# Layer 0's FFN in seven block products: where its weight sums are formed, and where layer 1's

## The chip, the cores and the metric

One core of one Trainium2 chip runs the whole program. The time is device microseconds of that core. The kernel before took 1684.92 us, the median of three runs (1684.33 to 1690.12). A core has TensorE (PE in the profile), VectorE (DVE), ScalarE (ACT), GpSimd (POOL) and SyncE (SP), which issues the DMA transfers here.

## The reference

Two layers. Each has a token mixer of four parallel head groups (spatial gating, a bidirectional recurrence, windowed attention, pooling) between an input and an output projection, and then a SwiGLU FFN. X is 512 tokens of 1024 channels, the context C 256 tokens; layer 1 no longer updates C. All is fp32. What matters here is the FFN, with a hidden width of 2816, and the modulation, which gives shift, scale and gate of each layer from one vector:

```python
FFN_HIDDEN = -(-(8 * D_MODEL) // (3 * 256)) * 256     # 2816

def modulate(h, shift, scale):
    return h * (1 + scale) + shift
...
def swiglu(h, w_in_, w_out_):
    gate, up = jnp.split(h @ w_in_, 2, axis=-1)
    return (jax.nn.silu(gate) * up) @ w_out_
...
    x = x + g_f * rms_norm(swiglu(modulate(rms_norm(x, norm_g[2]), sh_f, sc_f), w_ffn_in, w_ffn_out), norm_g[3])
```

## The kernel before

**Matmuls.** Weights and activations are split into a high and a low part, and one fp32 product is three matmuls (`mac3`: high by high, high by low, low by high). A hidden tile of 128 of the 2816 channels needs two weight units of 1024 x 128, one for gate and one for up; the kernel calls it a pair, and there are 22, numbered from 0. In dense form a pair is 2 x 8 x 3 = 48 matmuls of 512 columns.

**Seven block products.** In layer 1 (`'strassen': (1,)`), pairs 4 to 21 take another form: the gate and up weights are seen as a matrix of 2 x 2 blocks, the tokens as 2 x 2 blocks of half the channels and half the tokens (`Quarters`), and seven block products replace eight. A product is 4 x 3 matmuls of 256 columns, so a pair is 84 of these. The right sides of the products are formed once (`strassen_rhs`, L1513). The left sides need four sums of weight blocks per pair, each 128 x 512. They don't depend on activations, so the kernel forms all 18 pairs' sums early, in layer 0's FFN (`weight_sums`, L1541), and stores them in DRAM (`ws`): per pair four loads of 256 KB into buffers `sa_m`, four adds at L1556 (`'sad': 'PPVV'`, two on POOL and two on DVE) and four stores of 256 KB at L1565. `strassen_pair` (L1574) then loads them like weights.

**Weights.** All streamed weights go through a ring of seven buffers `wr` (128 x 1024, 512 KB), loaded from SP's queue, then ACT writes the high part `wh` (L408) and DVE or POOL the low part `wl` (L409). Prefetched units that are held go into `wt_m`.

**Background work.** `weights` and `strassen_pair` call `tick` (L455) for each unit, which adds `bg_rate` to a counter and runs a queued task for each whole 1. In layer 0's FFN the queue holds 32 tasks of layer 1's modulation (`mods_sums`; each one `wmod` load of 512 KB and two DVE accumulations `macc_m`, L675 and L677) with the sums' tasks strewn among them, at `bg_rate` 1.4 (`rate2`). What is left is run by `flush`, which `then` in `layer_end` calls ahead of layer 1's first norm, since that norm needs the modulation.

**Order.** A scheduler with a timeline of its own places the instructions of each engine, within the priorities that the program sets; each engine then runs its own list in order. SP's list holds every load and store, so a store that waits for an add holds up the loads behind it.

**Stages by the profile's time:** to about 100 us the start; 100 to 570 layer 0's X projection and mixers, with the context's FFN woven in; 570 to 690 the output projection and norm; 690 to 1049 layer 0's FFN; 1049 to 1062 the norm into layer 1; to 1300 layer 1's projection and mixers, among them the recurrence, whose head norm takes `bym` from POOL (L504); 1313 to 1672 layer 1's FFN. In the norm, `rmsv` (L561) and `rmsy` (L504) are the root mean squares, `rs_t` (L595) the gated branch, `sq_t` and `sq_m` (L529) the squares that are added up, `y` (L1456) the FFN's output tiles; "halves" are tiles of 256 of the 512 tokens.

The two lines that set the rate and the mix of tasks, in `mix` of `run`:

```python
            for i, f in enumerate(b):
                self.bg += a[i * len(a) // len(b):(i + 1) * len(a) // len(b)] + [f]
            self.bg_rate = T["rate2"]
```

Of the kernel before, what the change touches and what calls it, by code (L numbers as in the profile page):

```python
# [66 lines left out]
 'rate2': 1.4,  # L67
# [41 lines left out]
 'strassen': (1,),  # L109
 'fcs': ((0, 4), (4, 7), (7, 11), (11, 16), (16, 22)),  # L110
 'fco': 4,
 'fcp': (5, 1, 3),
 'wq': 2,
 'sad': 'PPVV',
 'slo': 'PVVPPVP',
# [147 lines left out]
class Build:  # L263
    def __init__(self, tc, es, I, out, dbg=None):
# [22 lines left out]
        self.sums = {}  # L287
        self.pre = deque()
# [1252 lines left out]
    def weight_sums(self, l, j0, j1):  # L1541

        nc = self.nc

        def load(j, box):
            for u in range(2):
                for v in range(2):
                    s = self.main.get("sa")
                    nc.sync.dma_start(out=s.t[:, 0:512].rearrange("p (a b) -> p a b", b=P), in_=self.I["wfi"][l, j, u][:, v * 4:v * 4 + 4])
                    box.append(s)  # L1550

        def form(j, box):
            a11, a12, a21, a22 = (s.t[:, 0:512] for s in box)
            box += [self.main.get("sb") for _ in range(2)]
            s1, s2 = (s.t[:, 0:512] for s in box[4:])
            tt = lambda c, o, a, b, op=ALU.subtract: self.e(c).tensor_tensor(out=o, in0=a, in1=b, op=op)  # L1556
            e = T["sad"]
            tt(e[0], s1, a21, a22, ALU.add)
            tt(e[1], a21, a11, a21)
            tt(e[2], s2, s1, a11)  # L1560
            tt(e[3], a12, a12, s2)
            d = self.dr.tile([P, 2, KT, P], F32, tag=f"ws{l}{j}", name=f"ws{l}{j}")
            self.sums[l, j] = d
            for i, x in enumerate((s2, s1, a21, a12)):
                nc.sync.dma_start(out=d[:, i // 2, i % 2 * 4:i % 2 * 4 + 4], in_=x.rearrange("p (a b) -> p a b", b=P))  # L1565
            for s in box:
                s.free()

        boxes = {j: [] for j in range(j0, j1)}
        tasks = [lambda: load(j0, boxes[j0])]  # L1570
        for j in range(j0, j1):
            if j + 1 < j1:
                tasks.append(lambda j=j: load(j + 1, boxes[j + 1]))
            tasks.append(lambda j=j: form(j, boxes[j]))  # L1574
        return tasks

    def strassen_pair(self, l, j, h, rhs, g, jj):
# [3 lines left out]
        raw = []  # L1581
        for src in (self.I["wfi"][l, j, 0], self.sums[l, j][:, 0], self.sums[l, j][:, 1], self.I["wfi"][l, j, 1][:, KT // 2:KT]):
            self.tick()
            r = self.wr.tile([P, UNIT], F32, tag="wr", name=self.name("wr"))
            k = src.shape[1]
            nc.sync.dma_start(out=r[:, 0:k * P].rearrange("p (a b) -> p a b", a=k), in_=src)
            raw.append(r)
        lhs = [r[:, i * 512:i * 512 + 512] for r in raw for i in range(2)][0:7]
# [6 lines left out]
        for i in range(7):  # L1595
# [258 lines left out]
    def run(self):  # L1854
# [37 lines left out]
        self.bg_rate = T["rate0"]  # L1892
        def flush_ctx():
# [42 lines left out]
        def mix():  # L1936
# [6 lines left out]
            a, b = list(self.bg), self.weight_sums(1, T["fcs"][0][1], HID)  # L1943
            self.bg.clear()
            for i, f in enumerate(b):
                self.bg += a[i * len(a) // len(b):(i + 1) * len(a) // len(b)] + [f]
            self.bg_rate = T["rate2"]
# [164 lines left out]
```

## Time and profile before

| | before |
|---|---|
| median of the runs | 1684.92 us |
| profiled execution, its own time | 1689.32 us |
| span of its instructions | 1687.2 us |
| mean granted TensorE clock | 0.967 of 2.4 GHz |
| busy: PE, DVE, ACT, POOL | 1604.0, 1089.6, 791.9, 739.8 us |
| DMA: moved, mean rate | 271.34 MB, 161 GB/s |

The span is one execution; the profiled run lies 4.40 us over the median, of which 2.12 us is outside the span. Busy matmul times overlap, since matmuls are pipelined: the pace of PE is read from the distance between starts, not from the duration of one.

### The profile page before, as it was taken

Reading aid. Unit: us, or ns where it says so; the run is one execution under the profiler, and the core shown is the slowest. Engines: PE = TensorE matmul, PEld = TensorE weight load, DVE = VectorE, ACT = ScalarE, POOL = GpSimd, SP = SyncE. Lnnn points to the kernel's source line nnn. Section 1 sums busy time; section 2 is a strip of 40 time slices with the busy share of each in tenths; the row PEclk is TensorE's granted clock in tenths of the full one; section 3 lists DMA queues with packets and bytes.
Section 4 is the critical chain, followed back from the end, with each engine's and each line's share of the span. In section 5 each row is a group of like instructions: output and inputs, shape, how many; then the busy total and the mean of one; then the engine's idle time right before and its main releaser. Section 6 shows DMA issues by size and latency. Waiting matters only on the chain.

```text
span 1687.2 us, 29374 instructions
## 1 busy us (share of the span) xinstructions
PE 1604.0 (95%) x10616; PEld 1401.4 (83%) x10616; DVE 1089.6 (65%) x2330; ACT 791.9 (47%) x1782; POOL 739.8 (44%) x779
## 2 busy tenths in 40 slices
PE   6999998999999998998999998999699999999997
PEld 2976877887899898876888888999569889999996
DVE  4887676647785668764775645667774755555664
ACT  3665356654345555222232343465374445555551
POOL 2431235554476565443543534422423564444553
PEclk9999998999999999999999999899699999999998
DMA  9854553354375323776896843122122234555441
GB/s 320 273 189 159 178 200 101 123 175 146 121 244 177 118 79 135 242 239 218 312 349 213 301 140 106 45 85 66 36 69 82 95 101 157 163 163 160 154 139 60
DMA packets 111584, 271.34 MB, mean 161 GB/s; under 512 B 13904, under 2 KB 22992, under 8 KB 111440
## 3 DMA queue, kind: packets, MB, share of 16 engines
q1 hardware_dynamic: 111440, 269.48, 48.8%
q8 instruction: 83, 1.36, 0.3%
q14 instruction: 61, 0.50, 0.1%
HBM read 244.27 MB, written 25.17 MB: 160 GB/s over the span
## 4 chain that ended last, share of the span: by engine, by line
PE 82%; DVE 10%; DMA 3%; issue 2%; ACT 1%; POOL 1%; SPq 0%; DVEq 0%; POOLq 0%; ACTq 0%
PE mm L470 19%; PE mm L471 19%; PE mm L472 19%; PE ms L634 2%; PE mx L471 2%; PE mx L472 2%; PE mx L1147 2%; PE mx L470 2%; PE mm L487 1%; PE mm L634 1%; PE mx L1399 1%; PE mm L488 1%; PE mm L492 1%; PE mx L1141 1%; PE mm L493 1%
## 5 line engine op out<-in xcount | busy, mean ns | idle before, releaser
L409 POOL TENSOR_TENSOR wl<-wr,wh 128x512 fp32r<-128x512 f32 (+2 forms) x268 | 361.3, 1353 | 439.7 <-ACT wh L408 387.5
L408 ACT ACTIVATE wh<-wr 128x512 fp32r<-128x512 f32 (+3 forms) x548 | 333.5, 617 | 438.6 <-PE mm L471 299.6
L409 DVE TENSOR_TENSOR wl<-wr,wh 128x512 fp32r<-128x512 f32 (+3 forms) x280 | 225.3, 807 | 124.8 <-ACT wh L408 120.7
L472 PE MATMUL mm<-hfh_m,wl 128*128 128x512 f32 (+1 forms) x320 | 124.3, 389 | 1.1 <-DVE wl L409 1.1
L470 PE MATMUL mm<-hfh_m,wh 128*128 128x512 f32 (+1 forms) x320 | 125.3, 392 | 0.0
L471 PE MATMUL mm<-hfl_m,wh 128*128 128x512 f32 (+1 forms) x320 | 124.2, 388 | 0.0
L471 PE MATMUL mm<-hfl_c,wh 128*128 128x256 f32 x352 | 100.8, 287 | 0.6 <-POOL hfl_c L582 0.6
L470 PE MATMUL mm<-hfh_c,wh 128*128 128x256 f32 x352 | 101.2, 288 | 0.0
L472 PE MATMUL mm<-hfh_c,wl 128*128 128x256 f32 x352 | 100.1, 285 | 0.0
L472 PEld LDWEIGHTS mm<-hfh_m,wl 128*128 128x128 f32 x320 | 60.1, 188 | 14.9 <-DVE wl L409 1.5
L470 PEld LDWEIGHTS mm<-hfh_c,wh 128*128 128x128 f32 x352 | 66.8, 190 | 6.6 <-issue 2.7
L677 DVE SCALAR_TENSOR_TENSOR macc_m<-wr,cs,macc_m 128x512 f32<-128x512 f32 x56 | 59.0, 1054 | 19.4 <-DMA wr<-in_wmod_dram 18.7
L471 PEld LDWEIGHTS mm<-hfl_m,wh 128*128 128x128 f32 x320 | 60.3, 188 | 13.0
L470 PEld LDWEIGHTS mm<-hfh_m,wh 128*128 128x128 f32 x320 | 60.2, 188 | 12.9
L471 PEld LDWEIGHTS mm<-hfl_c,wh 128*128 128x128 f32 x352 | 67.0, 190 | 2.4 <-issue 1.0
L472 PEld LDWEIGHTS mm<-hfh_c,wl 128*128 128x128 f32 x352 | 67.1, 191 | 1.0 <-issue 0.4
L470 PE MATMUL mm<-gh_m,wh 128*128 128x512 f32 x152 | 61.0, 402 | 6.2 <-ACT gh_m L411 6.2
L471 PE MATMUL mm<-gl_m,wh 128*128 128x512 f32 x152 | 60.8, 400 | 0.0
L472 PE MATMUL mm<-gh_m,wl 128*128 128x512 f32 x152 | 60.5, 398 | 0.0
L411 ACT ACTIVATE gh_m<-ft_m 128x512 fp32r<-128x512 f32 (+1 forms) x32 | 17.6, 551 | 77.1 <-DVE ft_m L1508 77.1
L470 PE MATMUL mx<-gh_m,wh 128*128 128x512 f32 x128 | 50.5, 396 | 0.9 <-ACT wh L408 0.7
L472 PE MATMUL mx<-gh_m,wl 128*128 128x512 f32 x128 | 50.5, 395 | 0.6 <-POOL wl L409 0.6
(722 smaller groups left out, 5365.1 us busy)
## 6 DMA issues: line engine op xcount, KB each, us to landing
wr<-in_wfi_dram SPq DMA_DIRECT2D x114, 512.0 KB, 4.0
wr<-in_wmod_dram SPq DMA_DIRECT2D x80, 512.0 KB, 4.4
wr<-in_wT_dram SPq DMA_DIRECT2D x42, 512.0 KB, 4.4
sa_m<-in_wfi_dram SPq DMA_DIRECT2D x72, 256.0 KB, 5.5
wr<-ws SPq DMA_DIRECT2D x36, 512.0 KB, 3.8
wr<-in_wo_dram SPq DMA_DIRECT2D x24, 512.0 KB, 4.1
wr<-in_wfo_dram SPq DMA_DIRECT2D x24, 512.0 KB, 3.8
ws<-sb_m SPq DMA_DIRECT2D x36, 256.0 KB, 5.4
```

The lines of the kernel that those rows point to most:

```text
L408: nc.scalar.activation(hi, src, AF.Copy)
L409: (eng or nc.vector).tensor_tensor(out=lo, in0=src, in1=hi.bitcast(F32), op=ALU.subtract)
L411: nc.scalar.activation(hi, src, AF.Copy, scale=scale)
L470: nc.tensor.matmul(out, lh, rh, start=first, stop=False, skip_group_check=more)
L471: nc.tensor.matmul(out, lh, rl, start=False, stop=False, skip_group_check=more)
L472: nc.tensor.matmul(out, ll, rh, start=False, stop=last, skip_group_check=more)
L487: nc.tensor.matmul(out, w.h[w0 + i], ah, start=f, stop=False)
L488: nc.tensor.matmul(out, w.l[w0 + i], ah, start=False, stop=False)
L492: nc.tensor.matmul(out[:, c], w.h[w0 + i], ah[:, c], start=f and q == 0, stop=False)
L634: nc.tensor.matmul(ps[o:o + 32, :], self.cs[:, k, :], ws[i], start=True, stop=True, tile_position=(0, o))
L677: nc.vector.scalar_tensor_tensor(out=t, in0=w, scalar=self.cs[:, k, s:s + 1], in1=t, op0=ALU.mult, op1=ALU.add)
L1147: nc.tensor.matmul(po[kv * 64:kv * 64 + 64, 0:256], stream.av.t[b][:, kv * 64:kv * 64 + 64], pts[kv].t[:, i * 256:(i + 1) * 256], start=i0 ...
```

## The change

Layer 0's FFN also takes the form of seven block products for pairs 4 to 21. Its 18 sums are formed by POOL alone (`'sap': 'PPPP'`), as tasks of a second queue (`bg2`) that starts with layer 0's X projection, at 0.35 tasks per tick. A task takes three buffers of the `wr` ring (two loads of 512 KB, one for results) and issues three stores (256, 512 and 256 KB).

Layer 1's sums are no longer formed in layer 0's FFN. Nine pairs (4, 6, ..., 20) are formed by POOL in layer 1's mixers, at 0.3 tasks per tick, the rest of the queue being run ahead of the output projection (`flush_sums`). The other nine are formed in place, in `strassen_pair`: it loads the two raw units, two adds go to POOL and two to DVE (`sad`), and there are no stores.

The modulation tasks stay in layer 0's FFN. The statement that set `bg_rate` to `rate2` is gone, and `rate2` is read nowhere else, so the rate there is `rate1`, 0.2, set earlier.

```diff
- 'rate2': 1.4,
+ 'rate2': 0.5,
...
- 'strassen': (1,),
+ 'strassen': (0, 1),
...
+ 'sums0': tuple(range(4, 22)),
+ 'sums1': tuple(range(4, 22, 2)),
...
+ 'sap': 'PPPP',
+ 'pre_l0': 0.35,
+ 'pre_f0': 0.17,
+ 'pre_l1': 0.3,
...
+        self.bg2_acc = self.bg2_acc + self.bg2_rate if self.bg2 else 0.0
+        while self.bg2_acc >= 1 and self.bg2:
+            self.bg2_acc -= 1
+            self.bg2.popleft()()
...
+    def form_sums(self, engines, first, second, both):
+
+        a11, a12, a21, a22 = first[:, 0:512], first[:, 512:1024], second[:, 0:512], second[:, 512:1024]
+        s2, s1 = both[:, 0:512], both[:, 512:1024]
+        tt = lambda i, o, a, b, op=ALU.subtract: self.e(engines[i]).tensor_tensor(out=o, in0=a, in1=b, op=op)
+        tt(0, s1, a21, a22, ALU.add)
+        tt(1, a21, a11, a21)
+        tt(2, s2, s1, a11)
+        return lambda: tt(3, a12, a12, s2)
...
+        def task(j):
+            first, second, both = self.raw_unit(self.I["wfi"][l, j, 0]), self.raw_unit(self.I["wfi"][l, j, 1]), self.raw_unit()
+            self.form_sums(T["sap"], first, second, both)()
...
+            nc.sync.dma_start(out=d[:, 0], in_=v(both))
+            nc.sync.dma_start(out=d[:, 1, 0:4], in_=v(second[:, 0:512]))
+            nc.sync.dma_start(out=d[:, 1, 4:8], in_=v(first[:, 512:1024]))
...
+        else:
+            second = self.raw_unit(self.I["wfi"][l, j, 1])
+            self.tick()
+            both = self.raw_unit()
+            then = self.form_sums(T["sad"], first, second, both)
...
         self.bg_rate = T["rate0"]
+        if 0 in T["strassen"]:
+            self.queue_sums(0, "pre_l0")
...
             self.mods_sums(1, (2, 4, 3, 5), pn, 1)
-            a, b = list(self.bg), self.weight_sums(1, T["fcs"][0][1], HID)
-            self.bg.clear()
-            for i, f in enumerate(b):
-                self.bg += a[i * len(a) // len(b):(i + 1) * len(a) // len(b)] + [f]
-            self.bg_rate = T["rate2"]
+            if 0 not in T["strassen"]:
+                self.queue_sums(1, "pre_f0")
 
         self.layer_end(0, X, p, pn, norm, proj, mix)
+        self.flush_sums()
...
         self.ph = 5
+        if 0 in T["strassen"]:
+            self.queue_sums(1, "pre_l1")
```

Three places of the engines' lists follow. The line numbers of the changed kernel are some 9 to 22 higher than those of the kernel before (L417 is L409, L477 is L456, L1477 is L1456, L698 is L677, L1566 is the sums' add).

POOL, in layer 0's X projection, about 110 to 180 us of the profile, before: `wl` is a weight's low part, `bys` of a head norm.

```order
L409 TENSOR_TENSOR wl_229_1771<-wr_227_1768,wh_228_1770 128x512
L504 TENSOR_TENSOR bys_116_1046<-bvs_115_1045,mhalf_94 128x4
L1196 MEMSET gs_c57_1431 128x256
L1218 MEMSET m_c59_1450 64x256
L409 TENSOR_TENSOR wl_247_1884<-wr_245_1881,wh_246_1883 128x512
L504 TENSOR_TENSOR bys_121_1072<-bvs_120_1071,mhalf_94 128x4
L409 TENSOR_TENSOR wl_266_1997<-wr_264_1994,wh_265_1996 128x512
```

And the same place in the changed kernel:

```order
L417 TENSOR_TENSOR wl_229_1771<-wr_227_1768,wh_228_1770 128x512
L1566 TENSOR_TENSOR wr_247_1885<-wr_246_1883 128x512
L525 TENSOR_TENSOR bys_116_1046<-bvs_115_1045,mhalf_94 128x4
L1217 MEMSET gs_c57_1431 128x256
L1239 MEMSET m_c59_1450 64x256
L1566 TENSOR_TENSOR wr_246_1883<-wr_245_1881,wr_246_1883 128x512
L1566 TENSOR_TENSOR wr_247_1885<-wr_247_1885,wr_245_1881 128x512
L417 TENSOR_TENSOR wl_250_1897<-wr_248_1894,wh_249_1896 128x512
L525 TENSOR_TENSOR bys_121_1072<-bvs_120_1071,mhalf_94 128x4
L1566 TENSOR_TENSOR wr_245_1881<-wr_245_1881,wr_247_1885 128x512
L417 TENSOR_TENSOR wl_269_2010<-wr_267_2007,wh_268_2009 128x512
```

Four adds of a task stand between the low parts that PE's next units need.

DVE, at the last output tiles of layer 0's FFN (1034 to 1045 us of the profile), before: `y` are the second halves of the tiles, `rs_t` the branch of the first half.

```order
L595 SCALAR_TENSOR_TENSOR rs_t27_11785<-y4_m321_9250,Gf00_8263,mx_1649_11772 128x256
L595 SCALAR_TENSOR_TENSOR rs_t27_11785<-y5_m322_9251,Gf00_8263,mx_1649_11772 128x256
L595 SCALAR_TENSOR_TENSOR rs_t28_11790<-y6_m323_9252,Gf00_8263,mx_1649_11772 128x256
L595 SCALAR_TENSOR_TENSOR rs_t28_11790<-y7_m324_9253,Gf00_8263,mx_1649_11772 128x256
L1456 TENSOR_TENSOR y4_m321_9250<-mm_1642_11661,y4_m321_9250 128x256
L596 TENSOR_TENSOR x2_m227_7444<-x2_m227_7444,rs_t26_11780 128x256
L596 TENSOR_TENSOR x4_m229_7446<-x4_m229_7446,rs_t27_11785 128x256
L1456 TENSOR_TENSOR y5_m322_9251<-mm_1643_11687,y5_m322_9251 128x256
```

And the same place in the changed kernel:

```order
L582 TENSOR_SCALAR rmsv_1889_13301<-ms_1888_13296 128x2
L698 SCALAR_TENSOR_TENSOR macc_m444_13409<-wr_1910_13412,cs_101,macc_m444_13409 128x512
L1477 TENSOR_TENSOR y4_m309_9188<-mm_1884_13206,y4_m309_9188 128x256
L698 SCALAR_TENSOR_TENSOR macc_m444_13409<-wr_1911_13416,cs_101,macc_m444_13409 128x512
L550 TENSOR_TENSOR sq_m415_12910<-sq_m415_12910,sq_e9_13226 128x256
L698 SCALAR_TENSOR_TENSOR macc_m444_13409<-wr_1911_13416,cs_101,macc_m444_13409 128x512
L1477 TENSOR_TENSOR y5_m310_9189<-mm_1885_13229,y5_m310_9189 128x256
L698 SCALAR_TENSOR_TENSOR macc_m444_13409<-wr_1912_13420,cs_101,macc_m444_13409 128x512
L708 TENSOR_TENSOR mod1_4623<-ms_1893_13332,bmod1_4599 128x4
L616 SCALAR_TENSOR_TENSOR rs_t25_13308<-y0_m305_9184,Gf00_8497,mx_1891_13305 128x256
L616 SCALAR_TENSOR_TENSOR rs_t25_13308<-y1_m306_9185,Gf00_8497,mx_1891_13305 128x256
```

The accumulations of the modulation now stand between the output tiles, and `rs_t` behind `y5` where it stood ahead of `y4`.

POOL, in the norm into layer 1 (1053 to 1060 us of the profile), before: `sq_t` is part of the sum that the norm's root waits for, `rmsy` the root.

```order
L529 TENSOR_TENSOR sq_t29_11816<-sq_t29_11816,sq_t32_11829 128x256
L529 TENSOR_TENSOR sq_m460_11395<-sq_m460_11395,sq_e10_11735 128x256
L504 TENSOR_TENSOR rmsy_1652_11840<-rmsv_1651_11839,mhalf_94 128x2
L753 MEMSET zp_m526_12072 128x1
L754 MEMSET zp_m526_12072 128x1
L504 TENSOR_TENSOR rmsy_1660_11932<-rmsv_1659_11931,mhalf_94 128x2
```

And the same place in the changed kernel:

```order
L550 TENSOR_TENSOR sq_t29_13451<-sq_t29_13451,sq_t31_13459 128x256
L1566 TENSOR_TENSOR wr_1942_13696<-wr_1941_13694 128x512
L550 TENSOR_TENSOR sq_t29_13451<-sq_t29_13451,sq_t32_13464 128x256
L1566 TENSOR_TENSOR wr_1941_13694<-wr_1940_13692,wr_1941_13694 128x512
L1566 TENSOR_TENSOR wr_1942_13696<-wr_1942_13696,wr_1940_13692 128x512
L417 TENSOR_TENSOR wl_1960_14070<-wr_1958_14067,wh_1959_14069 128x512
L525 TENSOR_TENSOR rmsy_1916_13475<-rmsv_1915_13474,mhalf_94 128x2
L1566 TENSOR_TENSOR wr_1940_13692<-wr_1940_13692,wr_1942_13696 128x512
```

The first task of layer 1's sums now stands among the norm's instructions; its load of `wr_1941` stands in SP's list behind the stores of the new X.

## Rows read from the trace of the kernel before

**Rows 1.** Page: busy times; then transfer rates of the span's 40 slices

```profile
PE 1604.0 (95%) x10616; PEld 1401.4 (83%) x10616; DVE 1089.6 (65%) x2330; ACT 791.9 (47%) x1782; POOL 739.8 (44%) x779
...
GB/s 320 273 189 159 178 200 101 123 175 146 121 244 177 118 79 135 242 239 218 312 349 213 301 140 106 45 85 66 36 69 82 95 101 157 163 163 160 154 139 60
```

**Rows 2.** Page: shares of the chain that ended last

```profile
PE 82%; DVE 10%; DMA 3%; issue 2%; ACT 1%; POOL 1%; SPq 0%; DVEq 0%; POOLq 0%; ACTq 0%
```

**Rows 3.** Stretches: length, busy PE, PEld, DVE, ACT, POOL, granted clock, DMA share, GB/s

```profile
100.00:240.00 140.00, 140.00 (x800) 102.78 (x797) 102.92 (x328) 73.46 (x180) 35.05 (x54) 1.00 0.53 179
240.00:300.00 60.00, 53.45 (x354) 46.45 (x354) 34.23 (x91) 35.24 (x100) 25.51 (x29) 0.86 0.33 101
300.00:385.00 85.00, 84.38 (x645) 69.70 (x642) 53.94 (x118) 48.89 (x128) 48.21 (x45) 0.98 0.50 154
...
1060.00:1200.00 140.00, 137.07 (x1076) 131.14 (x1074) 99.53 (x285) 75.38 (x181) 48.42 (x72) 0.98 0.21 64
1200.00:1300.00 100.00, 87.33 (x578) 69.28 (x578) 59.16 (x197) 54.29 (x161) 28.25 (x39) 0.87 0.17 54
1313.00:1672.00 359.00, 354.07 (x2548) 333.09 (x2549) 205.58 (x334) 176.92 (x348) 174.11 (x142) 0.99 0.42 133
```

**Rows 4.** Timeline of PE: start, duration; 512 columns, then 256 columns

```profile
747.97 0.40 PE L470 MATMUL mm<-hfh_m,wh 128*128 128x512 f32 x1
...
750.29 0.39 PE L471 MATMUL mm<-hfl_m,wh 128*128 128x512 f32 x1
...
1024.61 0.28 PE L470 MATMUL mm<-gh_m,wt_m 128*128 128x256 f32 x1
...
1025.20 0.28 PE L472 MATMUL mm<-gh_m,wt_m 128*128 128x256 f32 x1
```

**Rows 5.** The stall at 759 us: its window, and the chain's pieces before it

```profile
750.00:770.00 20.00, 12.71 (x50) 10.02 (x50) 13.15 (x17) 5.46 (x10) 5.09 (x4) 0.86 0.56 180
...
728.88 1.75 POOL sb_m L1556
...
731.53 5.47 DMA ws<-sb_m
...
758.98 3.62 DMA wr<-in_wmod_dram
```

**Rows 6.** Groups of instructions: busy and mean ns; idle before and releasers

```profile
L409 POOL TENSOR_TENSOR wl<-wr,wh 128x512 fp32r<-128x512 f32 x246 | 335.9, 1371 | 390.9 <-ACT wh L408 341.5 <-PE mx L1095 11.4 <-DMA wr<-ws 8.6
...
L1556 POOL TENSOR_TENSOR sa_m<-sa_m,sa_m 128x512 f32<-128x512 f32 x18 | 29.3, 1626 | 2.1 <-POOL sb_m L1556 0.8 <-PE mx L1329 0.5 <-DMA sa_m<-in_wfi_dram 0.2
L1556 POOL TENSOR_TENSOR sb_m<-sa_m,sa_m 128x512 f32<-128x512 f32 x18 | 27.5, 1528 | 50.1 <-DMA wr<-in_wfo_dram 9.9 <-DVE gl_m L412 8.9 <-DMA ws<-sb_m 8.7
```

**Rows 7.** Line L677: ns min/median/max

```profile
L677 DVE SCALAR_TENSOR_TENSOR macc_m<-wr,cs,macc_m x56: 735/752/1823, 677.6 to 944.4; 128x512 f32<-128x512 f32 x56
```

**Rows 8.** Stretches at the end of layer 0's FFN, columns as in Rows 3

```profile
1013.00:1022.00 9.00, 9.00 (x57) 8.04 (x57) 3.77 (x5) 3.26 (x6) 1.38 (x1) 1.00 0.59 187
1022.00:1041.00 19.00, 19.00 (x164) 19.00 (x163) 5.58 (x14) 4.29 (x10) 4.95 (x6) 1.00 0.09 32
1041.00:1061.00 20.00, 13.62 (x92) 13.06 (x92) 16.60 (x29) 8.78 (x21) 14.58 (x27) 0.83 0.46 139
```

**Rows 9.** Timeline of DVE, then POOL, in the norm into layer 1

```profile
1041.37 3.23 DVE L595 SCALAR_TENSOR_TENSOR rs_t<-y_m,Gf,mx 128x256 f32<-128x256 f32 x8 [2.15 <-PE mx L565]
...
1046.58 0.41 DVE L1456 TENSOR_TENSOR y_m<-mm,y_m 128x256 f32<-128x256 f32 x1
...
1059.28 0.16 DVE L561 TENSOR_SCALAR rmsv<-ms 128x2 f32<-128x2 f32 x1 [2.03 <-PE ms L554]
...
1053.36 0.87 POOL L529 TENSOR_TENSOR sq_t<-sq_t,sq_t 128x256 f32<-128x256 f32 x1
```

**Rows 10.** Page: DMA issues, KB each, us from issue to landing

```profile
wr<-in_wfi_dram SPq DMA_DIRECT2D x114, 512.0 KB, 4.0
```

**Rows 11.** The chain in layer 1's mixers, one of its POOL pieces

```profile
1207.55 1.03 POOL bym L504
```

More of the change, by code (lines that the diff above doesn't have):

```diff
@@ L287, in __init__ @@
         self.sums = {}
+        self.bg2 = deque()
+        self.bg2_rate = self.bg2_acc = 0.0
         self.pre = deque()
@@ L462, in tick, with queue_sums, flush_sums @@
             self.bg.popleft()()
+        self.bg2_acc = self.bg2_acc + self.bg2_rate if self.bg2 else 0.0
+        while self.bg2_acc >= 1 and self.bg2:
+            self.bg2_acc -= 1
+            self.bg2.popleft()()
+    def queue_sums(self, l, rate):
+        self.weight_sums(l, T[f"sums{l}"])
+        self.bg2_rate = T[rate]
+    def flush_sums(self):
+        while self.bg2:
+            self.bg2.popleft()()
     def flush(self, left=0):
@@ L1539, in strassen_rhs @@
         return out, [b11, b21, out[1], out[0], out[2], b22, out[3]]
-    def weight_sums(self, l, j0, j1):
-        nc = self.nc
[L1545 to L1575, printed above, removed]
@@ new lines, in form_sums, with raw_unit @@
+    def form_sums(self, engines, first, second, both):
[6 more added lines that the diff above has]
+        return lambda: tt(3, a12, a12, s2)
+    def raw_unit(self, src=None):
+        r = self.wr.tile([P, UNIT], F32, tag="wr", name=self.name("wr"))
+        if src is not None:
+            k = src.shape[1]
+            self.nc.sync.dma_start(out=r[:, 0:k * P].rearrange("p (a b) -> p a b", a=k), in_=src)
+        return r
@@ L1580, in strassen_pair @@
         n = h.half
-        raw = []
-        for src in (self.I["wfi"][l, j, 0], self.sums[l, j][:, 0], self.sums[l, j][:, 1], self.I["wfi"][l, j, 1][:, KT // 2:KT]):
-            self.tick()
[L1584 to L1588, printed above, removed]
+        first = self.raw_unit(self.I["wfi"][l, j, 0])
+        self.tick()
+        if (l, j) in self.sums:
+            d = self.sums[l, j]
+            both, second = self.raw_unit(d[:, 0]), self.raw_unit(d[:, 1])
+            self.tick()
+            last, s3, s4, then = self.raw_unit(self.I["wfi"][l, j, 1][:, KT // 2:KT])[:, 0:512], second[:, 0:512], second[:, 512:1024], None
+        else:
+            second = self.raw_unit(self.I["wfi"][l, j, 1])
+            self.tick()
+            both = self.raw_unit()
+            then = self.form_sums(T["sad"], first, second, both)
+            last, s3, s4 = second[:, 512:1024], second[:, 0:512], first[:, 512:1024]
+        lhs = [first[:, 0:512], first[:, 512:1024], both[:, 0:512], both[:, 512:1024], s3, s4, last]
         z, w, y = self.mm(), None, None
@@ L1600, in strassen_pair @@
                 y = self.mm()
+                if then:
+                    then()
             if i == 3:
```

5 lines of the change are left out of this document (added).

## The prediction

> **What bounds the kernel now.** I read the busy times first: PE is busy for 95% of the span, POOL for 44% [rows 1]. The chain that ended last runs through PE for 82% of the span, through DVE for 10% [rows 2]. So the kernel is bound by PE's count of matmuls, except at some places where PE waits for DVE, POOL or a load. Then the stretches: in the X projection and in layer 1's FFN PE has work all the time (140.00 of 140 us, 354.07 of 359), while the mixers' tails lose 6.5 us of 60 and 12.7 us of 100 [rows 3]. Fewer matmuls in layer 0's FFN therefore shorten the time one for one, and what decides is whether the work that moves into other stretches makes PE wait there.
>
> **Layer 0's FFN: the matmuls.** Starts lie 2.32 us apart over ten matmuls of 512 columns, so 0.232 us each, and 0.59 us over five of 256, so 0.118 us [rows 4]. A dense pair is 48 x 0.232 = 11.14 us, one in block products 84 x 0.118 = 9.91 us. 18 pairs save 18 x 1.23 = 22.1 us. Layer 1 already runs this form with PE at 354.07 us of 359 and DVE at 205.58 [rows 3], so I see no reason for another pace in layer 0.
>
> **Layer 0's FFN: what else leaves and comes.** The sums' adds and stores leave it. They stood behind its one large gap: from 750 to 770 us PE is busy for 12.71 us, with a mean granted clock of 0.86; the chain before it is a POOL add that came late, its store of 5.47 us, and loads of the modulation behind that store [rows 5]. That is 7.3 us of idle PE, and a little of the clock; I take 8 us as gained, with 4 as the low end, as some of the modulation's waits could remain. What comes is the forming of the right sides ahead of the first product: in the changed lists it stands behind four output tiles, and shares DVE with the last of the context's work. Layer 1's start has the same forming, and its whole stage loses only 4.9 us [rows 3]. I take 4 us, between 0 and 8. Sum of the stage: -22 - 8 + 4 = **-26 us** (-18 to -32).
>
> **Layer 0's projection and mixers: 72 more POOL adds.** A 128x512 POOL subtraction takes 1.37 us as a weight's low part, 1.53 and 1.63 us as a sum [rows 6]: four are 5.5 to 6.3 us, 18 tasks 99 to 114 us. POOL is busy for 35 of 140, 26 of 60 and 48 of 85 us between 100 and 385 us [rows 3], and the changed list holds some 9.5, 2.5 and 6 tasks there. That makes 62 to 68%, 66 to 69%, and 95 to 101% of the three stretches. The first two have room; the third is full, and POOL also makes low parts of weights and pieces of the mixers' chain there. Two other costs come with it: an add waits for its raw load, and what is queued behind it on POOL (low parts, for which PE waits) waits too; and the three stores wait for the adds in SP's list, with later loads behind them. The gap at 759 us is this pattern, and it came once in 18 tasks at a price of 7.3 us [rows 5]. Transfers: 18 x 2 MB over 285 us are 132 GB/s on top of 179, 101 and 154 [rows 3]; 311 at the most, under the 349 of the busiest slice [rows 1]. I take one such gap in 18 tasks, less what slack there is, as **+6 us**; 0 where the queues' lead hides it, 20 (nearly three gaps) where the full third stretch slides into the chain.
>
> **The junction of the layers.** With the rate left at 0.2, by the changed lists only 15 of the 32 modulation tasks run inside the FFN, and 17 are flushed into its last output tiles: 17 loads and 34 DVE accumulations. Nine of these accumulations stand ahead of the last chunk's first outputs, the others between them. An accumulation takes 0.75 us at the median and 1.82 us at the most [rows 7]; were one in four as slow as that, the mean would be 1.0 us, so 25 of them are 19 to 25 us. DVE is busy in the two stretches from 1013 to 1041 us for 3.8 + 5.6 = 9.4 of 28 us [rows 8], so 18.6 us are free: DVE ends there between 0 and 7 us late. The list now has `rs_t` behind the tile `y5`, which was evacuated at 1046.58 us by a DVE that was then busy; by PE's pace it would be there some 3 us after `rs_t`'s 1041.37 us [rows 9]. On POOL a sum's add stands ahead of a square `sq_t` that ran at 1053.36 us [rows 9], and that add waits for a raw load behind the stores of the new X; a load takes 4.0 us [rows 10]. Two or three POOL adds more (1.4 to 1.6 us each) stand ahead of the root. From 1041 to 1061 us PE is busy for 13.62 of 20 us and DVE for 16.60 [rows 8], and the norm's second `rmsv` comes at 1059.28 us [rows 9]: this chain has no cover, and PE's first projection waits for it. 3 for the order, 0 to 7 for DVE, 2 to 6 for POOL: 5 to 16 us, and I take **+10 us**.
>
> **Layer 1's mixers: 36 more POOL adds.** Nine tasks are 50 to 56 us of POOL. From 1060 to 1300 us POOL is busy for 48 + 28 of 240 us [rows 3], so there is room on the whole, but the list holds five tasks nearly back to back, some 28 us, just ahead of the recurrence's `bym`. That step lies on the chain with 1.03 us [rows 11], in the stretch where PE is already without work for 12.7 us of 100. A task ahead of it costs its remainder, up to 6 us; a second or third is possible. I take **+6 us**, 0 to 20.
>
> **Layer 1's FFN.** Nine pairs form their sums in place: two adds on POOL and two on DVE per pair, 27 us on POOL's 174 and some 20 to 25 on DVE's 206 of 359 us [rows 3]. Both stay under 65%. Raw loads fall from 1.75 MB to 1 MB per such pair. I take **+2 us**, 0 to 6.
>
> **The rule of the skill that speaks against it.** Rows first: a `macc_m`, whose tensors lie in SBUF, takes 0.735 us at the least and 1.823 us at the most [rows 7], and in the timeline the long ones lie beside POOL's adds. The Trainium skill (SBUF — State Buffer, section SBUF: two separate sides) says that DVE instructions with two SBUF inputs and POOL instructions take turns at a shared port pair, as an exclusive lock for the whole instruction. By that rule the two engines' times add up. In the third stretch of layer 0, DVE's 53.9 us, POOL's 48.2 and 33 to 38 more would need 135 to 140 us where 85 are, 50 us more. Yet the trace has DVE and POOL together at 102 us in those 85 with PE at 84.38 [rows 3], so by this row much of DVE's work there doesn't take turns. I keep it as a rival of its own.
>
> **The sum.** -26 + 6 + 10 + 6 + 2 = -2 us. Against the profiled run of 1689.32 us that is 1687.3; that run lies 4.40 us over the median of 1684.92 us, and against the median I forecast **1683 us**: no change. About 0.5%, 8.4 us, is what a measurement of this kernel can tell from none: 1676.5 to 1693.3.
>
> **The rivals.** (a) The gain mostly stays: POOL's adds in both mixers hide behind PE's lead (0 and 2 us, where the room by the busy times is real), the junction costs its low end, 5: -26 + 0 + 5 + 2 + 1 = -18, 1667 us. For it: POOL is idle for 56% of the span [rows 1], and PE's queue of ready weights is some units deep. Against it: the third stretch is full and the junction's chain is bare. (b) Slower: POOL becomes the bound where it stands in order ahead of the mixers' chain. Each gap costs 7.3 us; from six gaps in the two mixers (instead of under two) the gain of 26 is gone together with the junction's 10 and it is slower: -26 + 6 x 7.3 + 10 + 2 = +30, 1715 us; with four, +15, 1700 us. It decides for slower from -26 + 10 + 2 + g > 8.4, that is g = 22 us, three gaps. (c) The change doesn't do what its numbers say: `rate2` is never set, so the flush is a side effect. If DVE can't take the 34 accumulations between tiles, they cost in full after the outputs: 34 x 0.75 = 25 us instead of 10: +13, 1698 us. (d) DVE and POOL take turns, by the rule above: +50 in the third stretch: 1733 us.
>
> **Chances.** Forecast, within 0.5%: 0.38. (a) 0.36. (b) 0.16, (c) 0.08, (d) 0.02, all slower: 0.26. For the range I leave out (d), the upper half of (b) and the lowest of (a): 1661 to 1703 us. The terms' low ends alone give -32 + 0 + 5 + 0 + 0 = -27, 1658 us, which I hold too good to come together.
>
> **What would show it.** In the changed profile: starts of 0.118 us through layer 0's FFN and no gap like that at 759 us; its stage shorter by 18 to 32 us. POOL near 95% or more between 300 and 385 us, with PE idle behind a low part or a pooled sum. The norm into layer 1 with `rs_t` 3 to 10 us later after the last output tiles, and PE idle for over 15 us there. In layer 1's mixers PE idle behind `bym` that waits for a sum's add. Layer 1's FFN as long as before within 6 us. I am wrong if the FFN saves under 18 us, if POOL's adds leave PE's starts in layer 0's projection untouched, or if the junction loses under 5 us or over 16.

## The result, and the profile after

The changed kernel takes 1752.15 us, the median of four runs (1749.05 to 1755.13), against 1684.68 us before: a ratio of 1.0383, 95% interval 1.0358 to 1.0407. It is 67 us slower where I had forecast 2 us less. The span grew from 1687.2 to 1753.4 us.

The page of the changed kernel: busy times, then the granted clock (in tenths) and the transfer rates of the span's 40 slices.

```profile
span 1753.4 us, 32062 instructions
...
PE 1625.8 (93%) x11714; PEld 1467.7 (84%) x11714; DVE 1206.6 (69%) x2435; ACT 843.9 (48%) x1906; POOL 936.8 (53%) x920
...
PEclk8999998898999998989999998899889899999998
...
GB/s 319 254 251 234 270 271 256 135 281 235 181 193 217 179 55 186 76 67 173 192 178 185 169 242 274 167 161 159 192 13 109 115 48 123 140 136 134 121 125 67
```

Beside [rows 1]: POOL went from 739.8 to 936.8 us, DVE from 1089.6 to 1206.6. The sums' adds on POOL are these two groups of the changed kernel (count, busy us, mean ns), 174.5 us where the 36 of [rows 6] made 56.8:

```profile
L1566 POOL TENSOR_TENSOR wr<-wr,wr 128x512 f32<-128x512 f32 x90 | 125.7, 1408 | 1.8
...
L1566 POOL TENSOR_TENSOR wr<-wr 128x512 f32<-128x512 f32 x36 | 48.8, 1355 | 34.5 <-DMA wr<-in_wfi_dram 10.2 <-DVE bms L816 4.9 <-DVE gqX L1213 4.7
```

DVE lost 18 of its 36 sums' adds and is still busy for 117 us more. That is the first hint; 30 of these us are in layer 0's FFN, whose new form gives DVE 86 instructions more (rows below).

To compare stretches I cut both traces at the same instructions of PE: the first matmul that reads layer 0's normed X, the first of the output projection, of layer 0's FFN, of layer 1's projection, of layer 1's FFN, and the last of all.

| stretch, us | before | after | difference | forecast |
|---|---|---|---|---|
| layer 0's projection and mixers | 465.4 | 504.9 | +39.5 | +6 |
| its output projection and norm | 77.9 | 77.6 | -0.3 | 0 |
| layer 0's FFN and the norm into layer 1 | 419.1 | 422.5 | +3.4 | -16 (FFN -26, junction +10) |
| layer 1's projection, mixers, output projection | 253.9 | 277.0 | +23.1 | +6 |
| layer 1's FFN | 363.2 | 363.6 | +0.4 | +2 |

Stretches, here and below, are of one profiled execution of each kernel. Four lists with the same work in the first stretch (the changed kernel, and below those with `sums1` empty, with `rate2` set, and with both) take 504.9, 501.2, 504.0 and 503.3 us, so a difference of 3 or 4 us between two runs says little.

The same stretches of the changed kernel as windows; columns as in [rows 3].

```profile
99.00:603.90 504.90, 467.92 (x3220) 391.04 (x3219) 361.21 (x851) 242.52 (x592) 305.22 (x303) 0.94 0.66 225
...
681.50:1104.00 422.50, 398.51 (x3149) 389.53 (x3147) 294.46 (x470) 189.38 (x385) 204.76 (x184) 0.93 0.53 174
1104.00:1381.00 277.00, 243.43 (x1738) 218.72 (x1738) 189.49 (x497) 138.00 (x363) 135.21 (x153) 0.90 0.39 131
1381.00:1744.60 363.60, 355.91 (x2554) 334.04 (x2555) 230.03 (x355) 175.26 (x348) 204.08 (x160) 0.99 0.35 111
```

And three of the kernel before, in the same cut.

```profile
99.00:564.40 465.40, 454.39 (x3221) 384.39 (x3220) 315.49 (x849) 242.07 (x592) 206.95 (x231) 0.97 0.50 162
...
642.30:1061.40 419.10, 398.87 (x2050) 337.39 (x2049) 264.10 (x384) 135.64 (x260) 183.35 (x165) 0.98 0.66 222
1061.40:1315.30 253.90, 234.06 (x1733) 209.75 (x1732) 171.76 (x496) 138.73 (x363) 90.04 (x122) 0.94 0.21 66
```

The first row of each is the one to look at. POOL has 72 instructions more and 98 us more, as planned. DVE has the same work, 849 and 851 instructions, and takes 361.21 us for it instead of 315.49: 46 us more for nothing. ACT's 592 instructions take 242 us in both. Of PE's 39.5 us, 26 are idle time (37.0 us after, 11.0 before), and 13.5 are the same matmuls being busy for longer, at a mean granted clock of 0.94 in place of 0.97.

An example is line L1089 (L1068 before), a subtraction of 64x8 elements in the pooled mixer, both inputs in SBUF (the core's memory on the chip), and L1086, its larger neighbour (L1065 before). In layer 0's mixers, before and after, ns min/median/max:

```profile
L1068 DVE TENSOR_TENSOR pd_m<-pd_m,pz_m x8: 151/159/935, 385.8 to 392.1; 64x8 f32<-64x8 f32 x8
L1065 DVE SCALAR_TENSOR_TENSOR pd_m<-s_m,pinv,pz_m x4: 745/844/1435, 378.3 to 388.4; 64x512 f32<-64x512 f32 x4
```

```profile
L1089 DVE TENSOR_TENSOR pd_m<-pd_m,pz_m x8: 150/536/1216, 392.8 to 408.4; 64x8 f32<-64x8 f32 x8
L1086 DVE SCALAR_TENSOR_TENSOR pd_m<-s_m,pinv,pz_m x4: 915/1378/1672, 387.9 to 404.4; 64x512 f32<-64x512 f32 x4
```

These two are a small part of the 46 us. The `mxs` steps of the windowed attention (128x1 elements, 40 instructions) grew by 15 us, from 9.8 to 25.0 (12.2 with the memsets of a run below), and DVE's low parts `wl` of 128x512 by 8.

The timeline of POOL in the same place of the changed kernel (start, duration) shows sums' adds between the steps of that mixer and the low parts, without a pause:

```profile
396.12 1.74 POOL L1566 TENSOR_TENSOR wr<-wr 128x512 f32<-128x512 f32 x1
397.93 1.35 POOL L1067 TENSOR_TENSOR s_m<-s_m 64x512 f32<-64x512 f32 x1
399.36 2.88 POOL L1566 TENSOR_TENSOR wr<-wr,wr 128x512 f32<-128x512 f32 x2
402.20 1.27 POOL L417 TENSOR_TENSOR wl<-wr,wh 128x512 fp32r<-128x512 f32 x1
```

And PE waits for it; its longest waits in layer 0's projection and mixers (us in total, times, longest us), and the first of these in the kernel before, for which the same view lists no wait for a `wl` or `wh`:

```profile
PE mx L1091 <- DVE pd_m L1089: 5.8, 2, 3.9
PE mm L493 <- DVE wl L417: 5.1, 4, 2.0
PE mm L491 <- ACT wh L416: 4.9, 3, 2.2
```

```profile
PE mx L1070 <- DVE pd_m L1068: 1.8, 1, 1.8
```

A step of the chain that DVE did in 0.16 us at the median takes 0.54 us, a neighbour on POOL comes one add later, and PE, without work for that time, also falls in clock: 0.92 granted from 380 to 410 us, with PE busy for 21.36 of 30 us.

### The profile page after: what moved, and what is told of

The parts are those of the page before. It is cut to its first block, busy times and chain, and to the rows that moved or that the text cites. A ratio compares the mean times of both kernels' runs of the same rounds, so it can differ in the third digit from the quotient of the medians.

```text
span 1753.4 us, 32062 instructions
## 1 busy us (share of the span) xinstructions
PE 1625.8 (93%) x11714; PEld 1467.7 (84%) x11714; DVE 1206.6 (69%) x2435; ACT 843.9 (48%) x1906; POOL 936.8 (53%) x920
## 5 line engine op out<-in xcount | busy, mean ns | idle before, releaser
L417 POOL TENSOR_TENSOR wl<-wr,wh 128x512 fp32r<-128x512 f32 (+2 forms) x287 | 393.5, 1378 | 346.7 <-ACT wh L416 305.6
L417 DVE TENSOR_TENSOR wl<-wr,wh 128x512 fp32r<-128x512 f32 (+3 forms) x283 | 247.3, 878 | 100.7 <-ACT wh L416 96.3
L1566 POOL TENSOR_TENSOR wr<-wr,wr 128x512 f32<-128x512 f32 x90 | 125.7, 1408 | 1.8
L417 POOL TENSOR_TENSOR wl<-wq,wh 128x512 fp32r<-128x512 f32 (+1 forms) x40 | 53.4, 1336 | 75.2 <-ACT wh L416 57.9
L416 ACT ACTIVATE wh<-wq 128x512 fp32r<-128x512 f32 (+1 forms) x80 | 43.0, 543 | 65.7 <-PE mm L492 28.9
L515 PE MATMUL mx<-gh_m,wl 128*128 128x256 f32 x256 | 72.1, 282 | 2.1 <-DVE wl L417 2.1
L514 PE MATMUL mx<-gl_m,wh 128*128 128x256 f32 x256 | 72.0, 281 | 0.0
L513 PE MATMUL mx<-gh_m,wh 128*128 128x256 f32 x256 | 72.0, 282 | 0.0
L1566 POOL TENSOR_TENSOR wr<-wr 128x512 f32<-128x512 f32 x36 | 48.8, 1355 | 34.5 <-DMA wr<-in_wfi_dram 10.2
L698 DVE SCALAR_TENSOR_TENSOR macc_m<-wr,cs,macc_m 128x512 f32<-128x512 f32 x56 | 52.5, 939 | 10.3 <-DMA wr<-in_wmod_dram 9.7
L1477 DVE TENSOR_TENSOR y_m<-mx,y_m 128x512 f32<-128x512 f32 x48 | 32.9, 685 | 36.6 <-PE mx L493 33.0
L493 PE MATMUL mm<-gh_c,wl 128*128 128x256 f32 x176 | 49.6, 289 | 2.0 <-DVE wl L417 2.0
L492 PE MATMUL mx<-gl_m,wh 128*128 128x512 f32 x128 | 50.5, 394 | 0.7 <-DVE gl_m L420 0.7
```

The lines of the kernel that those rows point to most:

```text
L416: nc.scalar.activation(hi, src, AF.Copy)
L417: (eng or nc.vector).tensor_tensor(out=lo, in0=src, in1=hi.bitcast(F32), op=ALU.subtract)
L492: nc.tensor.matmul(out, lh, rl, start=False, stop=False, skip_group_check=more)
L493: nc.tensor.matmul(out, ll, rh, start=False, stop=last, skip_group_check=more)
L513: nc.tensor.matmul(out[:, c], w.h[w0 + i], ah[:, c], start=f and q == 0, stop=False)
L514: nc.tensor.matmul(out[:, c], w.h[w0 + i], al[:, c], start=False, stop=False)
```

## The experiments

Each changes the changed kernel by the lines shown. "The first stretch" is the one from layer 0's projection to its output projection.

**Where the sums are formed.** Two runs take one part of the change back each, a third both.

```diff
- 'sums0': tuple(range(4, 22)),      (x_in0, x_inall)
+ 'sums0': (),
- 'sums1': tuple(range(4, 22, 2)),   (x_in1, x_inall)
+ 'sums1': (),
```

> Only layer 0's 18 sums change: they are formed in place in layer 0's FFN (two adds on POOL, two on DVE per pair), nothing of them in its projection and mixers. Theory A, the adds in the mixers cost there (the stretch from 99 us to the output projection grew from 465.3 to 504.9 us): that stretch is back within 3 us of 465, layer 0's FFN stays at 420 to 428 us, and the time is 1711 to 1720 us. Rival B, the sums cost about the same wherever they stand, since DVE and POOL share what they wait for: the FFN grows by most of the 39 us, and the time stays over 1740 us.

> Only layer 1's nine sums of the mixers change: they too are formed in place in layer 1's FFN. Theory A: layer 1's mixers fall from 277 us to about 254 us, the FFN of layer 1 stays within 4 us of 364, the time is 1727 to 1736 us. Rival B: the FFN takes the 23 us over, the time stays over 1745 us. Rival C, the mixers of layer 1 are slow for the late weights and modulation from the junction and not for the sums: they stay over 270 us.

> All 36 pairs form their sums in place, none in the mixers. Theory A: both gains, 1685 to 1700 us, with what is left over the kernel before being the junction (some 11 us) and the start of layer 0's FFN. Rival B: over 1735 us.

Measured: 1733.63, 1730.49 and 1715.17 us, with the kernel before at 1688.08 us on that chip. The first stretch is 462.5 us in the first, layer 1's mixers 259.7 us in the second, so the adds do cost where they stand: 42 and 17 us. But layer 0's FFN goes to 442.7 us with its sums in place. Half of the 39 us was lost again there, which I had not expected, while layer 1's FFN takes its nine more in place for 4 us (367.5). With all in place (439.5, 258.6 and 366.9 us) the kernel is still 1.5% slower than before: 1.0153, 1.0128 to 1.0179. So neither theory holds alone: the adds cost 40 us in the mixers, and half as much in layer 0's FFN.

**The rate of the modulation.**

```diff
             self.mods_sums(1, (2, 4, 3, 5), pn, 1)
+            self.bg_rate = T["rate2"]
```

> Only the rate of the modulation tasks in layer 0's FFN changes: rate2 (0.5) is set there, so that they run among the pairs and fewer are flushed at its end. Theory A: the junction loses some 10 us less (PE's last wait for the modulation's accumulations, 8.9 us, is gone), 1738 to 1744 us. Rival: the wait of the norm stays, since POOL's adds and the late branch hold it, and the time stays at 1750 us or more.

Measured: 1747.5 us, a ratio of 1.0354 against 1.0383. That lies between the theory and the rival. The FFN with its norm fell by 8 us (414.6), but not where I had expected it: its first 90 us lose 14 us less (table further down). The tiles ended earlier, and then PE waited longer for the norm's squares. Waits of PE at that place, first of this run, then of the changed kernel:

```profile
PE ms L575 <- DVE sq_t L550: 15.6, 1, 15.6
```

```profile
PE ms L704 <- DVE mod L708: 8.9, 3, 4.8
```

The chain through `rs_t`, the new X and `sq_t` holds the norm either way. The flush alone was not the price of the junction.

**What in the adds costs.** Three runs keep layer 0's 18 tasks in the first stretch and change what they do: nothing but the transfers (with two buffers of the ring, not three), memsets of POOL in place of its adds, or the adds on DVE. The first two form no sums for layer 0.

```diff
-            self.form_sums(T["sap"], first, second, both)()
+            if l == 1:                                        (m_noadd, m_memset; m_noadd stores first in place of both)
+                self.form_sums(T["sap"], first, second, both)()
...
+            else:                                             (m_memset; four pairs of memsets)
+                g.memset(second[:, 0:1024], 0.0)
+                g.memset(both[:, 0:512], 0.0)
...
+            self.form_sums("VVVV" if l == 0 else T["sap"], first, second, both)()   (m_dve)
```

> As the changed kernel, but layer 0's tasks load their two units and store them again unchanged, without the four POOL adds and the third buffer (layer 0's weight sums are left out, so its FFN's numbers mean nothing). Theory A, POOL's adds cost in layer 0's projection and mixers: the stretch from 99 us to the output projection falls from 504.9 us to 465 to 472 us, the time is about 1715 us. Rival B, the transfers (36 MB more in that stretch), the ring's buffers and the stores in SP's list cost: the stretch stays over 490 us.

> As the changed kernel, but each POOL add of layer 0's tasks is replaced by two POOL memsets (128x1024 and 128x512, by the trace's 0.31 us for 256 and 0.52 us for 512 columns about 1.5 us together; layer 0's weight sums are left out). POOL's list, buffers, loads and stores stay; POOL reads nothing from SBUF in them. Theory A1, the adds hold up what is queued behind them on POOL: the stretch stays near 500 us. Theory A2, the adds slow DVE's instructions with two SBUF inputs (a 64x8 one of line L1089 took 0.54 us beside POOL and 0.16 us alone): the memsets leave DVE's alone, and the stretch falls to 465 to 480 us.

> As the changed kernel, but layer 0's 72 adds stand on DVE (0.68 us each alone, 49 us in all) and not on POOL. By A1 (POOL's queue) and A2 (DVE slowed by POOL) both, the loss moves to DVE's own queue: DVE is busy for some 71% of that stretch, so 49 us more make 81%; A2 with a DVE free of POOL's disturbance gives 475 to 490 us, less than the 504.9 us; if DVE's queue is as bad a place as POOL's, 500 us or more.

Measured: 1714.48, 1721.37 and 1727.83 us, with the kernel before at 1689.68 us on that chip. The first stretch of the three, as windows (columns as in [rows 3]):

```profile
99.00:564.30 465.30, 452.80 (x3231) 383.12 (x3230) 319.61 (x854) 242.27 (x593) 209.22 (x232) 0.97 0.71 242
```

```profile
99.00:576.50 477.50, 458.52 (x3223) 385.88 (x3222) 318.98 (x851) 241.63 (x592) 302.52 (x373) 0.97 0.70 237
```

```profile
99.00:579.40 480.40, 452.13 (x3217) 382.59 (x3216) 363.90 (x921) 242.11 (x592) 213.96 (x231) 0.98 0.70 236
```

The transfers cost nothing: 242 GB/s, and the stretch as long as before. The memsets keep POOL as busy as the adds did (302.52 against 305.22 us), and DVE's time falls back from 361 to 319 us; the stretch is 477, 12 us over the 465 without adds, where the adds made it 40 over. So of the 40 us some 12 go with POOL's list, the third buffer and the loads and stores that wait for it, and 28 with what POOL's reading does to DVE. (The scheduler places each kernel anew, so these two numbers are of three lists that are not quite the same.) On DVE the adds cost 15 us: DVE has 70 instructions more and 44 us more, and its other instructions take no more time together than before (311 us against 316).

The single instructions say the same: the median of line L1089 is 160 ns with the transfers alone, and with the memsets

```profile
L1089 DVE TENSOR_TENSOR pd_m<-pd_m,pz_m x8: 151/162/717, 396.0 to 407.4; 64x8 f32<-64x8 f32 x8
```

The traces also tell where the time is lost, if the same matmuls are compared with the kernel before:

| loss of PE in the first stretch, us | by the matmul that stood at 263 us | between those of 360 and 404 us | whole stretch |
|---|---|---|---|
| adds on POOL (changed kernel) | 20 | 20 | 40 |
| memsets on POOL | 12 | 3 | 12 |
| adds on DVE | 14 | 0 | 15 |
| transfers alone | 1 | -1 | 0 |

The 12 us that need no read by POOL are lost at the first place, and the adds cost about as much there when DVE does them, so there it is not POOL's reading that costs most. The loss at the second place, where the pooled mixer stands, comes with POOL's adds alone. (Between and behind the two places each list gains or loses a few us more.)

The memset is 0.53 us for 512 columns and 0.95 us for 1024. The Trainium skill (SBUF — State Buffer, section SBUF: two separate sides) says that DVE instructions with two SBUF inputs take turns only with POOL instructions that read SBUF. The memsets, which read nothing, agree: 319 us of DVE. (The prediction named the rule without that condition.)

**How the loss goes with the number of adds.**

```diff
- 'sums0': tuple(range(4, 22)),
+ 'sums0': tuple(range(4, 22, 2)),
- 'pre_l0': 0.35,
+ 'pre_l0': 0.175,
```

> Nine of layer 0's 18 sums formed by POOL in its projection and mixers, at half the rate (0.175), so over the same stretch; the other nine in place in layer 0's FFN. What it tells is the stretch from 99 us to the output projection (465.4 us before, 504.9 with 18 tasks, 465.0 with none). Theory A, each add slows DVE's work beside it: the loss goes with the number of adds, 482 to 488 us. Rival, the loss comes from POOL being full between 300 and 385 us (79.6 of 100 us busy there in the changed kernel): with half the adds it falls to a quarter or less, under 475 us.

Measured: 1744.25 us. The first stretch:

```profile
99.00:574.10 475.10, 455.06 (x3218) 383.39 (x3218) 342.85 (x846) 241.94 (x592) 259.52 (x266) 0.97 0.59 198
```

It is 475.1 us, 10 us over its length without adds, for half the adds: between what the two theories gave. DVE's time fell too: 342.85 us, 27 over the 316 of before, so it does go with the adds (46 for 72). The loss of PE does not: 10 against 40. By the matmul that stood at 263 us, 3 us are lost with nine tasks, and 5 more between those of 360 and 404 us, where it was 20 and 20. The rows show two parts: PE is idle for 11.0 us before, 20.0 with nine tasks and 37.0 with 18, and it is busy for 454.4, 455.1 and 467.9 us, at a mean granted clock of 0.97, 0.97 and 0.94. So with the full set a lower clock comes on top of longer waits, and with nine tasks it does not. That the slowed DVE work costs once the slack of the stretch is used up fits this, but no run shows the slack.

**What holds the in-place sums in layer 0's FFN.** From the run with all sums in place, one change each.

```diff
- 'sad': 'PPVV',                                    (x_inall_v)
+ 'sad': 'VVVV',
...
+            self.bg_rate = T["rate2"]              (x_inall_r2, in mix)
```

> All sums in place, as in the run that had all 36 pairs in place (layer 0's FFN 439.5 us, layer 1's 366.9), but all four adds of a pair on DVE and none on POOL. Theory A, in layer 0's FFN the in-place sums cost 21 us more in its middle since POOL's two adds hold up DVE's two and slow its other work (DVE waited 18.3 us for POOL's adds there): the middle loses 8 to 16 us less, layer 0's FFN is at 424 to 432 us. Rival, DVE is simply too full there (232 of 300 us busy, with the modulation's accumulations): layer 0's FFN gets longer, 445 us or more.

> All sums in place and the modulation at rate2 (0.5): 32 tasks inside layer 0's FFN, where 15 ran with the rate of 0.2. Theory, DVE is what the in-place sums and the modulation share: the middle of layer 0's FFN loses 8 us or more over the 27.0 us that it lost at rate 0.2, the end of it loses less than its 19.5 us, and the sum of both is not lower. Rival, the flush at the end is the larger evil: layer 0's FFN falls by 8 us or more.

Measured: 1710.34 and 1733.04 us, with the kernel before at 1689.70 us on that chip. Layer 0's FFN is 429.3 us in the first, 10 less than with POOL's two adds, though DVE takes all 72; the middle of it loses 21 us instead of 27, its start 27 instead of 32. In the second it is 453.4 us, 14 more, and the middle loses 51. Both went as the theory had it, but for the middle in the first, 6 us less where at least 8 were expected. The windows of layer 0's FFN, with two adds on each engine, four on DVE, and with more modulation:

```profile
641.70:1081.20 439.50, 404.02 (x3148) 392.95 (x3146) 337.98 (x505) 187.49 (x384) 258.33 (x216) 0.93 0.42 136
```

```profile
639.80:1069.10 429.30, 395.40 (x3148) 386.68 (x3148) 359.26 (x541) 187.72 (x384) 208.58 (x180) 0.95 0.42 139
```

```profile
641.90:1095.30 453.40, 400.29 (x3149) 389.91 (x3148) 354.11 (x505) 187.71 (x384) 263.00 (x216) 0.95 0.41 132
```

DVE busy alone does not tell: the middle run has the most and the shortest time. The first and the third have the same 505 instructions of DVE, and in the third they take 16 us more. What differs is that its modulation, whose instructions read two SBUF tensors, runs among the pairs, beside POOL's adds, and not at the end. That this is the cause fits the runs above and is not shown by one of its own.

**The junction without sums and without a flush.** Both lines of `sums1` and `rate2` above.

> As the changed kernel, with both things taken from the junction of the layers at once: layer 1's sums all in place (no POOL adds in the norm into layer 1) and the modulation at rate2 (nothing flushed into the last tiles). With one of the two alone PE's starts lost some 22 us from the last output tiles on in each case, as with both. Theory: either one alone holds the norm; without both, layer 0's FFN with its norm falls from 413.6 and 414.6 us to 402 to 407 us, and the time is 1717 to 1724 us. Rival: the late end comes from the order of the tiles and the branch, which neither touches: 412 us or more.

Measured: layer 0's FFN with its norm is 410.7 us, less than with either alone (413.6 and 414.6), and between what the theory and the rival gave; the time is 1733.12 us, a ratio of 1.0256, the same as with `sums1` alone (1.0253). From the last tiles on PE loses 14.9 us; before it was 10.9, with either alone 19.6 and 20.7. So sums and flush each hold the norm when the other is gone, and 4 us stay that are neither.

**A version with layer 0's FFN dense.** Three attempts to keep layer 1's seven products and form its sums better than the kernel before does.

```diff
- 'strassen': (0, 1),
+ 'strassen': (1,),
...
+            self.bg_rate = T["rate2"]         (rate2: 1.0 in v_l1in, 0.8 in the others)
...
- 'sums1': tuple(range(4, 22, 2)),
+ 'sums1': (),                              (v_l1in)
+ 'sums1': tuple(range(4, 22)),             (v_all, with 'pre_f0': 0.3)
```

> Layer 0's FFN dense as in the kernel before, and layer 1's 18 sums formed in place in its FFN; the modulation tasks at rate 1.0. Theory A: layer 0's FFN loses the gap at 759 us (7 to 10 us less), layer 1's FFN costs 4 us more as it did with all sums in place (366.9 us against 363.2), so 3 to 6 us under the kernel before. Rival: the in-place sums cost as much as in layer 0 (some 20 us), so slower by 10 us or more.

> Layer 0's FFN dense as in the kernel before; nine of layer 1's sums formed by POOL alone in that FFN (0.17 tasks per tick), the other nine in place, modulation at rate 0.8. Theory: POOL has room there (164 of 370 us busy, with the old sums in it), the gap at 759 us goes, and the layer 1 FFN with nine in place stays at 364 us as in the changed kernel: layer 0's FFN at 411 to 415 us, 4 to 8 us under the kernel before. Rival: POOL's adds slow DVE there too, no gain or a loss.

> As the last one, with all 18 sums formed by POOL alone in layer 0's dense FFN (0.3 tasks per tick), none in place. Theory: 72 adds, some 100 us of POOL in 370 us, still fit; PE's starts lose under 5 us in the FFN, the time is 3 to 8 us under the kernel before. Rival: late tasks fall into the norm into layer 1 and cost 5 us or more there.

Measured, with the kernel before beside them: ratios 1.0042 (1.0023 to 1.0061), 1.0023 (1.0012 to 1.0034) and 1.0021 (1.0011 to 1.0032). None beats the kernel before. In the first the FFN of layer 0 does fall to 412.1 us, the 7 us of the gap, and layer 1's FFN gives 9 back (372.4). In the second PE loses 7.7 us between 760 and 780 us, as it did in [rows 5] (FFN 418.0). In the third it loses only 1.9 us there, but 11 us between 880 and 920 us, and the FFN with its norm is 426.0 us. So sums formed by POOL alone still leave a gap; in the first, without sums, none of that size is left (2.5 us between 760 and 780).

## Why the prediction was wrong

**Layer 0's projection and mixers (+6, measured +39.5): the step that failed.** I counted POOL's time and its place in the list, which the memsets put at 12 us, inside my 0 to 20. What I had priced at nothing is what the adds do to DVE: 28 us. The mechanism, POOL's reads slowing DVE, stood in the prediction as rival (d): I had the rule in hand and set it aside for a wrong reason. That DVE and POOL were busy for 102 of 85 us [rows 3] shows that not all of DVE's work takes turns with POOL. It does not show that none does. [rows 7] showed a factor of 2.5 between the fastest and the slowest `macc_m`, and the slowest stood beside a sum's add on POOL. Of the 18 that took over 1.1 us, though, 8 stood beside such adds and 10 beside POOL's low parts alone, so it is POOL's subtractions in general that the row spoke of. From this the price could have been bounded, between nothing and the 99 to 114 us of the adds, in DVE's time; the run shows 46. The rival (d) had the right mechanism, a chance of 0.02, and a wrong size: it took all of DVE's work as affected (+50 in the third stretch alone). Its 1733 us, the nearest to the measured time, are in part luck: the loss lay in two places, one at the end of that stretch and one before 263 us, and what the clock and the other stages lost was in none of its terms. POOL was not full either: it is busy for 79.62 of the 100 us from 300 to 400, where my sign was 95%.

**Layer 1's mixers (+6, measured +23.1).** The range, 0 to 20, was just too short. Taking the nine tasks out gives 17 us back. Whether it is `bym` behind an add, as I had it, or DVE's small instructions slowed, was not tested there; PE's wait for what follows `bym` (`ht_m`, L821) grew only from 8.1 to 11.8 us. DVE was slowed there too: its 497 instructions take 189.49 us where 496 took 171.76, and with the nine tasks out:

```profile
1091.90:1351.60 259.70, 235.95 (x1737) 213.03 (x1737) 173.67 (x499) 139.43 (x364) 92.53 (x123) 0.92 0.20 65
```

The 5.8 us that stay without sums (259.7 against 253.9 us) I have not settled.

**Layer 0's FFN (-26, measured -6 without its norm).** The matmuls came as worked out. Adding each matmul's undisturbed distance between starts [rows 4] (0.06 us for those of few columns) gives 381.6 us before and 361.4 after: 20.2 us saved where I had 22.1. What PE loses beyond that, by place, from the same sums:

| loss of PE in layer 0's FFN, us | first 90 us | granted clock in them | middle | last 45 us |
|---|---|---|---|---|
| before | 14.1 | 0.96 | 12.5 | 10.9 |
| after | 33.1 | 0.81 | 8.2 | 20.0 |
| after, adds of layer 0 on DVE | 25.8 | 0.92 | 5.9 | 21.0 |
| after, rate2 set | 19.1 | 0.96 | 13.7 | 20.7 |
| after, rate2 set, layer 1 in place | 19.3 | 0.96 | 15.4 | 14.9 |
| after, all sums in place | 31.6 | 0.83 | 27.0 | 19.5 |

The middle, where the gap at 759 us stood, loses 4 us less, the low end of what I took. The start was put at +4 (0 to 8) and is +19: the term of this sum that was mis-sized. There the forming of the right sides meets the context's states, and PE gets small matmuls between waits. The granted clock there, as windows:

```profile
740.00:750.00 10.00, 8.15 (x47) 6.14 (x45) 5.41 (x11) 2.00 (x4) 8.35 (x19) 0.83 0.42 141
750.00:760.00 10.00, 10.00 (x37) 7.02 (x37) 3.16 (x11) 1.63 (x3) 4.45 (x4) 0.50 0.09 26
760.00:770.00 10.00, 10.00 (x72) 10.00 (x72) 7.40 (x9) 3.87 (x7) 6.38 (x5) 0.81 0.10 28
```

From 750 to 760 us PE has work for the whole ten us at a granted clock of 0.50, the lower of its two levels, 1.2 GHz; in the ten before it PE was busy for 8.15 us. It did 37 matmuls, of 256 and 65 columns, where 72 stand in the next ten. I had no term for that. By the table, some 14 of the 19 us come with the lower clock: with `rate2` set the clock of these 90 us is 0.96 as before, and 19.1 us are lost in place of 33.1; the other 5 come without it. In the whole stage PE is busy for 398.51 us after and 398.87 before: the 20 us of matmuls saved are spent again, at a mean granted clock of 0.93 in place of 0.98. What brought the clock down there is not shown. Layer 1's start, which I took as the nearest row, has no context work in it.

**The junction (+10, measured +9.1)** was right in size, but not by its parts, and so in part by luck: I took 3 for the order, 0 to 7 for the flush and 2 to 6 for POOL; the runs show that taking out the flush alone gains nothing there (20.7), nor taking out the sums alone (19.6), both together 5 us: the two cover each other, where I had added them.

**Layer 1's FFN (+2, measured +0.4)** was right. **The rivals:** none of their times (1667 to 1733 us) reached the measured 1752. (b), POOL as the bound ahead of the chain, is the nearest of those with a real chance, and is a part of the loss (12 us); (c) is wrong, since with `rate2` set the time falls by 5 us only; (a) needed room on POOL, and there was room, but DVE paid for its use.

## What to carry to other kernels

Work moved to an idle engine is not free if it slows the engine on the chain, as POOL's adds slowed DVE here: look for the same instruction's shortest and longest time in the trace before, see what ran beside the long ones, and price the moved work by that. A stage that saves PE's time one for one keeps it only if its start, its end and its helpers (here sums, modulation, norms) have room too: layer 0's FFN saved 20 us of matmuls and gave it back in the first 90 and the last 45 us and outside. And a rule that speaks against a change should be given its chance by what it predicts for single instructions, not be put away by a total.

## What the runs showed of the hardware

A POOL subtraction of 128x512 with both inputs in SBUF slows DVE's instructions with two SBUF inputs beside it: one of 64x8 from 0.16 to 0.54 us at the median. 72 such subtractions cost DVE 46 us. A POOL memset of the same size in sum does not (DVE 319 against 316 us). 36 MB of transfers more in 465 us, at 242 GB/s in place of 162, cost PE nothing measurable. PE lost four times as much for twice the adds (40 and 10 us); of the 30 us between the two, 17 are idle time and 13 busy time, with a granted clock of 0.94 in place of 0.97. What stays open: what PE waits for at the first place of loss (12 us with memsets, 14 with the adds on DVE), what brought the clock down at the start of layer 0's FFN, and the 5.8 us that layer 1's mixers lose without sums.
